# Side work paced closer together, and buffers and weights placed elsewhere, in a hybrid decoder step

## The chip, the cores and the metric

The kernel runs on one core of a Trainium2 chip. The metric is the device time of one execution in microseconds (us). A core has TensorE (PE, matmuls, with a separate record PEld for weight loads), VectorE (DVE), ScalarE (ACT), GpSimd (POOL) and SyncE (SP, which issues most DMAs). Each engine takes its instructions in the order of the built program and waits on semaphores for the others. Intermediate results of PE go to accumulators (`acc`, `tp`, `po`), from which DVE and ACT fetch them.

## The reference

One layer of a decoder with 1024 model dimensions, for a prompt of 2048 tokens and 8 samples of one token each, all in fp32:

```python
ada = silu(c) @ w_ada + b_ada
shift, scale, gate = split(ada, 3)
hn = rmsnorm(x, g_norm) * (1 + scale) + shift
xa, za, q, k, v, glr, zg = split(hn @ w_in)
...
xc = conv_b + sum(xp[:, j:j + T] * conv_w[j] for j in range(4))   # RG-LRU group, from xa
gx, ga = sigmoid(blockdiag(xc, w_gate_x)), sigmoid(blockdiag(xc, w_gate_a))
h = linear_recurrence(a(ga), mult * gx * xc)
y_lru = h * silu(za)
...
o, S = gated_linear_attention(q, k, v, log_alpha(glr))            # GLA group, 4 heads
y_gla = rmsnorm(o) * silu(zg)
...
x = x + gate * (concat(y_lru, y_gla) @ w_out)
y = rmsnorm(x, g_final)
```

The outputs are `y` for prompt and samples and the new states (recurrence, convolution, attention). So there are two large products, the input projection `hn @ w_in` and the output projection by `w_out` (2048 x 1024), and everything between is per head or per tile of 128 channels.

## The kernel before, in words

**Arithmetic.** A product of fp32 matrices is made of three matmuls in a reduced-precision type (fp32r): both operands are split into a high part, a cast on ACT, and a low part, a subtraction on DVE (`hh` and `hl` for the data, two halves of `w` for the weights), and high x high, high x low and low x high are summed in an accumulator. Split weights are made once and stored in DRAM (`parts`).

**Stages.** Tokens are worked in two halves. In the first half, tokens 0 to 1023, the attention heads run in the order 3, 0, 1, 2 and after each head some LRU tiles. From about 598 to 709 us stands a stage that computes the second half's gate columns (`zg` of three heads, `za` and `xa` of two tiles) in a Strassen-like way: `seven` makes a 2 x 2 block product of seven products instead of eight (five of them with sums or differences of blocks on one side). The data's sums come from `sums` (`so`, `ra`), the weights' differences from `pair_weights`. `gates_ahead` and `gates_seven` put the results through SiLU (ACT L1096, DVE L1097) into buffers `zs` and store them (`zgd`), `lru_seven` runs a whole LRU tile with its scan (DVE L1294) and output (DVE L1312). Then follows the second half: heads, and after each one LRU tile; tiles 6 and 7 come last. Last comes the output phase, from about 1190 us, again with seven products per block pair (L1792), whose weights `w<-wd` (L1656) and data `a<-mixd` (L1908) are loaded from DRAM and, where not stored split, cast on ACT (L1642).

**Side work and its pacing.** Three jobs run in the background: `ada_gate` (the adaLN gate), `pair_weights` (five pairs of column blocks of `w_in`: load at L749, two groups of differences at L753, four split copies at L758 and L759 with their stores at L763) and `out_weights` (16 steps over `w_out`: load at L809, two multiplications by the gate and four differences at L827, for every second group of four steps two split copies at L831 and L832, and stores to `wd` and `wd2` at L845 and L836). A step of `out_weights` uses one buffer `r`, so the next load can land only when the last step's stores have been read. `out_weights` begins when both other jobs are done (`ready`). None of this is placed by hand: each part ends with `after(units, fn)`, which puts its successor on a heap, due when a clock has advanced by so many units; the main loops call `tick`, which advances the clock and runs what is due. So the delays written in the jobs set how many steps fit into a stage. `with behind(V)` puts an instruction after the last that DVE has been given so far. `out_weights` pauses for the stage of sevens, whose pool `sp` takes the place of its buffers (pool `hp`): `lru_last_a` sets a stop flag and `close_sp` resumes. A scheduler decides the final order on each engine from this program.

At the end of the second half's loop stand these lines (L1624); what is left of `out_weights` is run there, ahead of the output phase's first loads and, in SP's and ACT's order, of the gates of LRU tile 6 (PE L1275 to L1277, whose input `xh` ACT casts at L1255):

```python
    while outw["busy"]:
        heapq.heappop(pend)[2]()
```

**Buffers of the stage of sevens.** `new_zs` hands out four shared buffers of pool `lp`, used by the gates and by the LRU tiles alike. Pool `sp` has slots s0 to s5; `fs4` holds the blocks' sums in s0, s1 and s2. Weights of a product are a tile of 2 x 1088 floats per partition that holds two operands, loaded by `operand` at float 0 and 576, or, for products whose data is a sum (`shifted`), at 48 and 560; `ra` starts at float 48 of a row of 1088.

The other lines that matter below: the projections' weight loads L302, PE L650 to L652 and L335 to L337 (projection matmuls), L1354 (eviction of the LRU input), L1514 (the matmul of `product`), L1528 (an eviction between two of the seven products).

Of the kernel before, what the change touches and what calls it, by code (L numbers as in the profile page):

```python
# [54 lines left out]
def hybrid_kernel(ctx, tc, i, o):  # L55
# [685 lines left out]
    def pair_weights(n=0):  # L741

        cols = zpairs()
        if n == len(cols):
            ready("pairs")
            return
        r = hp.tile([P, 2, KT, P], F32, tag="tr", name="tr")
        for a, col in enumerate(cols[n]):
            SP.dma_start(r[:, a], i["w_in"][0, :, col:col + P].rearrange("(k p) n -> p k n", p=P))  # L749
        b11, b21, b12, b22 = r[:, 0, :4], r[:, 0, 4:], r[:, 1, :4], r[:, 1, 4:]  # L750

        def sub(x, y, z):
            return lambda: V.tensor_tensor(x, y, z, op=OP.subtract)  # L753

        def split(k, x):
            def f():
                t = hp.tile([P, 4, P], F32R, tag="th", name="th", bufs=2)
                S.copy(t, x)  # L758
                V.tensor_tensor(x, x, t.bitcast(F32), op=OP.subtract)  # L759

                def store():
                    for u, y in enumerate((t.bitcast(F32), x)):
                        SP.dma_start(twd[n, k, :, u], y.rearrange("p k n -> p (k n)"))  # L763

                after(0.5, store)
            return f

        def one(ops):
            if not ops:
                after(1, lambda: pair_weights(n + 1))  # L770
                return
            with behind(V):
                for f in ops[0]:
                    f()
            after(0.5, lambda: one(ops[1:]))

        after(1.5, lambda: one([[sub(b11, b12, b11), sub(b12, b22, b12)], [sub(b22, b22, b11), sub(b21, b21, b22)]]
                               + [[split(k, x)] for k, x in enumerate((b11, b22, b12, b21))]))

    def out_weights(s0=0):  # L780


        def begin(s):
            q = s // 8
            outw["busy"] = True

            g = hp.tile([P, 2, 256], F32, tag="g", name="g")
            bt = hp.tile([P, 2, 256], F32, tag="t", name="bt")
            SP.dma_start(g, dram(gated, (8 + 32 * q) * 256, [[0, P], [64 * 256, 2], [1, 256]]))
            SP.dma_start(bt, dram(i["b_ada"], 2 * D + q * 256, [[0, P], [512, 2], [1, 256]]))  # L790
            r = load(s)

            def add():
                with behind(V):
                    V.tensor_tensor(g, g, bt, op=OP.add)
                after(0.5, lambda: step(s, r, g))

            after(4, add)

        def where(s):  # L800

            return s // 8, s // 4 % 2, s % 4

        def load(s):
            q, f, m = where(s)
            r = hp.tile([P, 2, 2, 256], F32, tag="r", name="r")
# [12 lines left out]

        def step(s, r, g):  # L820
            t = hp.tile([P, 3, 256], F32, tag="t", name="t")
            b11, b12, b21, b22 = r[:, 0, 0], r[:, 0, 1], r[:, 1, 0], r[:, 1, 1]
            q, f, m = where(s)
            c = slice(q * 256, q * 256 + 256)

            def op(*a):
                return lambda: V.tensor_tensor(*a[:3], op=a[3])  # L827

            def split(n, x):
                p = hp.tile([P, 2, 256], F32R, tag="p", name="p", bufs=2)  # L830
                S.copy(p[:, 0], x)  # L831
                V.tensor_tensor(p[:, 1], x, p[:, 0].bitcast(F32), op=OP.subtract)  # L832

                def store2():
                    for h in range(2):
                        SP.dma_start(wd2[n, :, h, m, c], p[:, h].bitcast(F32))  # L836

                after(1.5, store2)

            def store():  # L840

                for x, ops in ((r[:, 0], (B11, T1)), (r[:, 1], (B21, B22)), (t, (T2, T3, T4))):
                    for n, k in enumerate(ops):
                        if not (f and k in (B22, T4)):
                            SP.dma_start(wd[f, k, :, m, c], x[:, n])  # L845
                if outw["stop"] or s == 15:
                    outw["busy"], outw["next"] = False, s + 1
                elif s % 8 < 7:
                    after(1, lambda: again(s + 1, g))
                elif q == 0:  # L850
                    after(1, lambda: begin(s + 1))

            one([[op(r[:, 0], r[:, 0], g, OP.mult)], [op(r[:, 1], r[:, 1], g, OP.mult)],
                 [op(t[:, 1], b22, b12, OP.subtract), op(b12, b12, b11, OP.subtract)],
                 [op(t[:, 0], b22, b12, OP.subtract), op(t[:, 2], b21, t[:, 0], OP.subtract)]]
                + ([[lambda: split(0, b22)], [lambda: split(1, t[:, 2])]] if f else []), lambda: after(1, store))

        def again(s, g):
            r = load(s)
            after(1.5, lambda: step(s, r, g))  # L860

        begin(s0)
# [560 lines left out]
        ra[:] = [new_ra(F32) for _ in range(2)]  # L1423

    def new_ra(dt):
        return wp.tile([P, 1088], dt, tag="wr", name="ra")[:, 48:1072].rearrange("p (k t) -> p k t", k=2)

    def new_so(n):
        return sp_.tile([P, 4, 512], F32R, tag=f"s{n}", name="so")
# [54 lines left out]
    operands = []  # L1484

    def operand(src, shifted):

        if operands:
            c = 560 if shifted else 576
            w = operands.pop()  # L1490
        else:
            c = 48 if shifted else 0
            w = wp.tile([P, 2, 1088], F32R, tag="w", name="w", bufs=3)
            operands.append(w)
        w = w[:, :, c:c + 512]
        SP.dma_start(w.bitcast(F32), src)
        return w.rearrange("p u (k n) -> p u k n", k=4)
# [22 lines left out]
    def seven(n, use, c2, first=False):  # L1520
# [6 lines left out]
        y = acc()  # L1527
        S.copy(y, x)  # L1528
        if first:
            product(x, ZB21, n, False)  # L1530
            use(0, 0, x)
            g = acc()
            product(g, ZT4, n, True)
            gs = xp.tile([P, 512], F32, tag="f512", name="gs")
            S.copy(gs, g)
        e = acc()
# [25 lines left out]
    def gates_seven(n):  # L1562

        h = HEADS[1 + n]

        def use(dt, s, ps):
            z = new_zs()
            silu(z, ps)
            S.dma_start(zgd[2 * h + dt][:, s * 512:s * 512 + 512], z)

        seven(n, use, lambda s: new_zs(), n == 0)

    def lru_seven(j):
        xa_load, xa_new, xa_unit, out = lru_units(1, seven=True)
# [630 lines left out]
```

## Time and profile before

| | |
|---|---|
| three runs | 1521.42, 1521.81, 1523.98 us; median 1521.81 |
| the profiled execution | 1517.38 us, of which 1515.6 us is the span |
| mean granted clock of TensorE | 0.977 |
| chain that ended last | PE 78%, DVE 8%, ACT 5%, DMA 5% |
| `pair_weights` copies (ACT L758) | 20, from 134.0 to 334.3 us |
| `out_weights` multiplications (DVE L827) | 32 in 16 steps, from 405.9 to 1139.6 us |
| stage of sevens (PE L1514) | 599.6 to 708.9 us |
| first matmul of the output phase (PE L1792) | 1190.49 us |

The span is the time from the first to the last instruction of the profiled execution; all times of rows are from its start. A row of a timeline has the start, the duration, engine, line and operation, the output and input tiles, a count where neighbours were put together, and in brackets how long the engine had been idle before it and what released it. A row of waits reads: engine and instruction that waited, what released it, total us, times, longest. The page shows the span in 40 slices of 37.9 us, a digit being tenths of busy time.

### The profile page before, as it was taken

The numbers are of one execution on the slowest core, as the hardware profiler recorded it, in microseconds if no ns is written. First come the engines' busy times: TensorE is split into PE (matmuls) and PEld (weight loads), VectorE is DVE, ScalarE is ACT, GpSimd is POOL, SyncE is SP. The second block draws the span as 40 slices with busy tenths as digits, with TensorE's granted clock in tenths as the row PEclk, the third lists the DMA queues.
The fourth block names the chain that finished last, engine by engine and source line by source line (L and its number), as shares of the span: only waits on it lengthen the run. The fifth ranks groups of instructions, "written<-read, shape, count | busy, mean of one in ns | idle before, by whom it ended". The sixth has DMA issues, their size and how long they took to land.

```text
span 1515.6 us, 23410 instructions
## 1 busy us (share of the span) xinstructions
PE 1429.4 (94%) x8693; PEld 1249.2 (82%) x8693; DVE 1052.1 (69%) x2471; ACT 692.4 (46%) x1253; POOL 30.1 (2%) x44
## 2 busy tenths in 40 slices
PE   8999999999999999998999999999905999999998
PEld 6888889989899887777999999999804887778886
DVE  5767666765765687744387785868746896588886
ACT  4654535553552567334345555354405632144332
POOL 1200000000000002000000000000000100000000
PEclk9999999999999999999999999999956999999999
DMA  9656766764554634767557465664563658793452
GB/s 328 247 174 222 258 201 210 239 221 158 180 181 150 233 126 146 253 215 253 198 181 228 139 201 157 202 203 166 162 198 125 257 190 296 241 353 131 153 170 112
DMA packets 206135, 305.31 MB, mean 201 GB/s; under 512 B 13570, under 2 KB 143778, under 8 KB 203581
## 3 DMA queue, kind: packets, MB, share of 16 engines
q1 hardware_dynamic: 171317, 282.58, 55.6%
q10 hardware_dynamic: 34352, 20.19, 4.3%
q8 instruction: 68, 1.11, 0.3%
q0 software_dynamic: 352, 1.05, 0.2%
q14 instruction: 46, 0.38, 0.1%
HBM read 188.51 MB, written 115.33 MB: 200 GB/s over the span
## 4 chain that ended last, share of the span: by engine, by line
PE 78%; DVE 8%; ACT 5%; DMA 5%; issue 2%; SPq 1%; POOL 0%; DVEq 0%; ACTq 0%; POOLq 0%
PE acc L1792 12%; PE acc L650 10%; PE acc L652 10%; PE acc L651 10%; PE tp L1792 8%; PE acc L1514 5%; PE acc L335 4%; PE acc L336 4%; PE acc L337 4%; PE po L1044 1%; DMA r<-in_w_out_dram 1%; PE tp L1130 1%; DVE tg L1294 1%; PE tp L1010 1%; PE acc L1275 1%
## 5 line engine op out<-in xcount | busy, mean ns | idle before, releaser
L650 PE MATMUL acc<-hh,w 128*128 128x512 f32 (+3 forms) x1096 | 383.4, 350 | 1.8 <-DMA w<-parts 1.5
L651 PE MATMUL acc<-hl,w 128*128 128x512 f32 (+3 forms) x1096 | 372.9, 340 | 0.7 <-DVE hl L202 0.6
L652 PE MATMUL acc<-hh,w 128*128 128x512 f32 (+3 forms) x1096 | 372.5, 340 | 0.0
L650 PEld LDWEIGHTS acc<-hh,w 128*128 128x128 f32 x1096 | 206.2, 188 | 20.9 <-DVE f L973 1.8
L651 PEld LDWEIGHTS acc<-hl,w 128*128 128x128 f32 x1096 | 206.3, 188 | 19.0 <-DVE hl L202 1.9
L652 PEld LDWEIGHTS acc<-hh,w 128*128 128x128 f32 x1096 | 206.1, 188 | 17.4 <-issue 0.4
L1792 PE MATMUL acc<-w,a 128*128 128x512 f32 (+1 forms) x792 | 184.8, 386 | 0.0
L1792 PEld LDWEIGHTS acc<-w,a 128*128 128x128 f32 x792 | 146.8, 188 | 33.2 <-issue 3.4
L335 PE MATMUL acc<-w,hh 128*128 128x256 f32 (+1 forms) x508 | 145.4, 286 | 4.1 <-DVE zs L1097 4.0
L337 PE MATMUL acc<-w,hl 128*128 128x256 f32 (+1 forms) x508 | 143.4, 282 | 0.2 <-DVE hl L225 0.2
L336 PE MATMUL acc<-w,hh 128*128 128x256 f32 (+1 forms) x508 | 143.2, 282 | 0.0
L1792 PE MATMUL tp<-w,a 128*128 128x512 f32 x564 | 136.0, 391 | 0.0
L1792 PEld LDWEIGHTS tp<-w,a 128*128 128x128 f32 x564 | 105.2, 188 | 26.8 <-issue 5.2
L335 PEld LDWEIGHTS acc<-w,hh 128*128 128x128 f32 x508 | 96.3, 190 | 6.5 <-DVE zs L1097 4.2
L337 PEld LDWEIGHTS acc<-w,hl 128*128 128x128 f32 x508 | 96.7, 190 | 0.4 <-DVE hl L225 0.4
L336 PEld LDWEIGHTS acc<-w,hh 128*128 128x128 f32 x508 | 96.2, 189 | 0.1
L1096 ACT ACTIVATE zs<-acc 128x512 f32<-128x512 f32 (+3 forms) x73 | 36.8, 505 | 119.9 <-PE acc L652 104.4
L1275 PE MATMUL acc<-xh,wg 128*128 128x512 f32 (+3 forms) x80 | 31.2, 392 | 57.8 <-ACT xh L1255 57.1
L1642 ACT CAST a<-s 128x512 fp32r<-128x512 f32 x61 | 36.5, 619 | 95.8 <-issue 36.2
L1238 DVE SCALAR_TENSOR_TENSOR cv<-xa,vecT,cv 128x512 f32<-128x512 f32 (+2 forms) x120 | 75.7, 638 | 5.9 <-ACT cv L1236 5.5
L1097 DVE SCALAR_TENSOR_TENSOR zs<-zs,acc 128x512 f32<-128x512 f32 (+3 forms) x73 | 41.5, 568 | 51.4 <-ACT zs L1096 51.4
L1275 PEld LDWEIGHTS acc<-xh,wg 128*128 128x128 f32 x80 | 15.6, 197 | 63.7 <-ACT xh L1255 57.4
(373 smaller groups left out, 2555.1 us busy)
## 6 DMA issues: line engine op xcount, KB each, us to landing
parts<-w SPq DMA_DIRECT2D x37, 1024.0 KB
w<-parts SPq DMA_DIRECT2D x28, 1024.0 KB
wr<-in_w_in_dram SPq DMA_DIRECT2D x44, 512.0 KB
a<-mixd SPq DMA_DIRECT2D x63, 256.0 KB
w<-wd SPq DMA_DIRECT2D x12, 1024.0 KB
w<-twd SPq DMA_DIRECT2D x20, 512.0 KB
mixd<-zs ACTq DMA_DIRECT2D x34, 256.0 KB
wada<-in_w_ada_dram SPq DMA_DIRECT2D x16, 512.0 KB
```

Source lines behind the costliest of these rows:

```text
L335: PE.matmul(ps, hh[:, kt, c], hi[:, kt % 4], start=kt == 0, stop=False)
L336: PE.matmul(ps, hh[:, kt, c], lo[:, kt % 4], start=False, stop=False)
L337: PE.matmul(ps, hl[:, kt, c], hi[:, kt % 4], start=False, stop=kt == KT - 1)
L650: PE.matmul(ps[:, :n], hi[:, kt], a, start=kt == 0, stop=False)
L651: PE.matmul(ps[:, :n], hi[:, kt], b, start=False, stop=False)
L652: PE.matmul(ps[:, :n], lo[:, kt], a, start=False, stop=kt == KT - 1)
L1096: S.activation(z, ps, AF.Tanh, scale=0.5)
L1097: V.scalar_tensor_tensor(z, z, 1.0, ps, op0=OP.add, op1=OP.mult)
L1238: V.scalar_tensor_tensor(cv[:, cq], xa[:, cq.start + k:cq.stop + k], cw[k], cv[:, cq], op0=OP.mult, op1=OP.add)
L1275: PE.matmul(ps, wgh[:, g], xh[:, c], start=True, stop=False)
L1514: PE.matmul(ps, w[:, u, k], x[v][k], start=start and (k, u, v) == (0, 0, 0), stop=(k, u) == (3, 1), skip_group_check=True)
L1792: PE.matmul(ps, t[:, u, k], w[:, v, k, c], start=(q < 3 or ps is own) and (k, u, v) == (0, 0, 0), stop=(k, u) == (3, 1), skip_group_check= ...
```

## The change

1. In `pair_weights` the four split copies are issued two at a time, and the next pair begins at once instead of after 1 unit. In `out_weights` the two multiplications are issued together, then the four differences together, then both split copies together; the waits before the stores of split copies (1.5 to 0.5 units), before the stores (1 to 0.5) and before the next step (1 to 0.5) are shorter.
2. In `gates_seven`, for all gates but the first head's, results go to a tile `zq` of four turns in slot s2 of pool `sp` instead of the shared buffers.
3. Weights of products with sums, and `ra`, start eight floats later.
4. In `seven` for the first head, the product ZT4 is written ahead of ZB21.

```diff
@@ pair_weights
             if not ops:
-                after(1, lambda: pair_weights(n + 1))
+                pair_weights(n + 1)
                 return
...
-        after(1.5, lambda: one([[sub(b11, b12, b11), sub(b12, b22, b12)], [sub(b22, b22, b11), sub(b21, b21, b22)]]
-                               + [[split(k, x)] for k, x in enumerate((b11, b22, b12, b21))]))
+        halves = [split(k, x) for k, x in enumerate((b11, b22, b12, b21))]
+        after(1.5, lambda: one([[sub(b11, b12, b11), sub(b12, b22, b12)], [sub(b22, b22, b11), sub(b21, b21, b22)],
+                                halves[:2], halves[2:]]))
@@ out_weights
-                after(1.5, store2)
+                after(0.5, store2)
...
-                    after(1, lambda: again(s + 1, g))
+                    after(0.5, lambda: again(s + 1, g))
                 elif q == 0:
-                    after(1, lambda: begin(s + 1))
+                    after(0.5, lambda: begin(s + 1))
...
-            one([[op(r[:, 0], r[:, 0], g, OP.mult)], [op(r[:, 1], r[:, 1], g, OP.mult)],
-                 [op(t[:, 1], b22, b12, OP.subtract), op(b12, b12, b11, OP.subtract)],
-                 [op(t[:, 0], b22, b12, OP.subtract), op(t[:, 2], b21, t[:, 0], OP.subtract)]]
-                + ([[lambda: split(0, b22)], [lambda: split(1, t[:, 2])]] if f else []), lambda: after(1, store))
+            one([[op(r[:, 0], r[:, 0], g, OP.mult), op(r[:, 1], r[:, 1], g, OP.mult)],
+                 [op(t[:, 1], b22, b12, OP.subtract), op(b12, b12, b11, OP.subtract),
+                  op(t[:, 0], b22, b12, OP.subtract), op(t[:, 2], b21, t[:, 0], OP.subtract)]]
+                + ([[lambda: split(0, b22), lambda: split(1, t[:, 2])]] if f else []), lambda: after(0.5, store))
@@ new_ra
-        return wp.tile([P, 1088], dt, tag="wr", name="ra")[:, 48:1072].rearrange("p (k t) -> p k t", k=2)
+        return wp.tile([P, 1088], dt, tag="wr", name="ra")[:, 56:1080].rearrange("p (k t) -> p k t", k=2)
@@ operand
-            c = 560 if shifted else 576
+            c = 568 if shifted else 576
...
-            c = 48 if shifted else 0
+            c = 56 if shifted else 0
@@ seven
         if first:
+            g = acc()
+            product(g, ZT4, n, True)
             product(x, ZB21, n, False)
             use(0, 0, x)
-            g = acc()
-            product(g, ZT4, n, True)
@@ gates_seven
+        def new():
+            if n == 0:
+                return new_zs()
+            zturn[0] += 1
+            return zq[0][:, zturn[0] % 4]
+
         def use(dt, s, ps):
-            z = new_zs()
+            z = new()
...
-        seven(n, use, lambda s: new_zs(), n == 0)
+        if n == 1:
+            zq[:] = [sp_.tile([P, 4, 512], F32, tag="s2", name="zq")]
+        seven(n, use, lambda s: new(), n == 0)
```

More of the change, by code (lines that the diff above doesn't have):

```diff
@@ L1482, in sums @@
             drips.append(lambda n=n, u=u: step(n, u))
-    operands = []
+    operands, zq, zturn = [], [], [0]
     def operand(src, shifted):
         if operands:
-            c = 560 if shifted else 576
+            c = 568 if shifted else 576
             w = operands.pop()
         else:
-            c = 48 if shifted else 0
+            c = 56 if shifted else 0
             w = wp.tile([P, 2, 1088], F32R, tag="w", name="w", bufs=3)
```

## The prediction

> **What bounds the kernel now.** I read the page from the top, then the waits, then the stretches where the waits sit.
>
> ```profile
> span 1515.6 us, 23410 instructions
> PE 1429.4 (94%) x8693; PEld 1249.2 (82%) x8693; DVE 1052.1 (69%) x2471; ACT 692.4 (46%) x1253; POOL 30.1 (2%) x44
> PE   8999999999999999998999999999905999999998
> ...
> PEclk9999999999999999999999999999956999999999
> ```
>
> PE is busy 94% of the span and 9 in nearly every slice, so the kernel is bound by TensorE except where a slice is lower: one slice is 0 and the next 5, and the granted clock drops there and there alone. The waits of PE name it:
>
> ```profile
> PE acc L1275 <- ACT xh L1255: 57.1, 1, 57.1
> PE acc L335 <- DVE zs L1097: 4.0, 1, 4.0
> PE tp L209 <- DVE x L181: 2.2, 3, 1.7
> ```
>
> One wait of 57.1 us, one of 4.0 us, then nothing over 2.2 us in total. So a change that leaves the matmuls as they are can win some 61 us at two places, and crumbs elsewhere. The table of stretches (time, PE, PEld, DVE, ACT, POOL busy, granted clock, DMA share, GB/s) shows what the rest has to spare:
>
> ```profile
> 200.00:300.00 100.00, 99.86 (x631) 90.50 (x630) 69.08 (x152) 46.70 (x85) 0.00 (x0) 1.00 0.65 209
> ...
> 900.00:1000.00 100.00, 98.55 (x774) 94.41 (x774) 74.57 (x237) 49.95 (x103) 0.00 (x0) 1.00 0.62 193
> ...
> 1100.00:1150.00 50.00, 0.00 (x0) 0.00 (x0) 20.50 (x43) 3.24 (x8) 0.00 (x0) 0.50 0.63 206
> ```
>
> From 1100 to 1150 us PE does nothing while DVE works 20.5 of 50 us and ACT 3.2. What runs there is on DVE:
>
> ```profile
> 1098.92 1.52 DVE L827 TENSOR_TENSOR r<-r,g 128x512 f32<-128x512 f32 x2 [4.21 <-DMA r<-in_w_out_dram]
> ...
> 1138.59 0.69 DVE L827 TENSOR_TENSOR r<-r,g 128x512 f32<-128x512 f32 x1 [3.76 <-DMA r<-in_w_out_dram]
> ```
>
> These are the last six of the 16 steps of `out_weights`, run one after another by the loop that empties the heap when the second half ends. Each step is load, wait some 4 us, compute 3 to 4 us, store, and the next load needs the buffer: (1138.59 - 1098.92) / 5 = 7.9 us a step. Then come the loads and casts for the output phase, and only then the gates of tile 6:
>
> ```profile
> 1145.73 0.32 SPq L1656 DMA_DIRECT2D w<-wd  x1
> ```
>
> ```profile
> 1150.84 1.14 ACT L1642 CAST w<-w 128x512 fp32r<-128x512 f32 x2 [8.18 <-DMA w<-wd]
> ```
>
> ```profile
> 1096.18 0.34 PE L652 MATMUL acc<-hh,w 128*128 128x384 f32 x1
> 1153.63 1.01 PE L1275 MATMUL acc<-xh,wg 128*128 128x384 f32 x2 [57.11 <-ACT xh L1255]
> ...
> 1160.77 0.39 PE L650 MATMUL acc<-hh,w 128*128 128x264 f32 x1
> ```
>
> **The change, part by part. Part 1, the steps sooner.** The work per step is unchanged. Only its ticks of the pacing clock go: a pair's split pieces go two at a time, a pair's successor comes at once, and an out-weight step takes two or three turns instead of four to six, with shorter delays. In the built program seven of the 16 steps lie ahead of the second half instead of three, and the nine others lie spread through it at what are now 766 to 1035 us, 25 to 37 us apart. The last store of out-weights is SP instruction 529 of 705, in front of the last weight loads of the projections; the emptying loop finds nothing. Six steps leave the gap.
>
> What takes their place: PE has its last matmul of tile 6's projection at 1096.18 + 0.34 = 1096.5, and the next projection starts at 1160.8, 64.2 us later. In between stand 18 gate matmuls, 12 of 384 columns and 6 of 264. At full clock neighbouring projection matmuls follow one another at:
>
> ```profile
> 1094.97 0.33 PE L651 MATMUL acc<-hl,w 128*128 128x384 f32 x1
> 1095.14 0.33 PE L652 MATMUL acc<-hh,w 128*128 128x384 f32 x1
> ...
> 1161.61 0.28 PE L650 MATMUL acc<-hh,w 128*128 128x264 f32 x1
> 1161.73 0.28 PE L651 MATMUL acc<-hl,w 128*128 128x264 f32 x1
> ```
>
> 12 x 0.17 + 6 x 0.12 = 2.8 us. The gates' inputs still pass through ACT, which now has casts of out-phase weights mixed in: from the built order, with a cast at half of the 1.14 us above, I estimate some 8 us of ACT work between 1091 and 1099, and so 2.4 us of waiting for PE. So 5.2 us instead of 64.2: **-59.0**. The bounds are 2.8 us, no wait at all (-61.4), and 2.8 + 2.4 + 8.2 = 13.4 us, ACT blocked for a whole weight load as in the row at 1150.84 (-50.8). I take the inner value: in the built order the `w<-wd` load stands behind the load below, waits only on transfers long done, and has some 15 us before its cast.
>
> ```profile
> 1075.46 0.53 SPq L302 DMA_DIRECT2D w<-parts  x1
> 1088.29 0.53 SPq L302 DMA_DIRECT2D w<-parts  x1
> ```
>
> What it costs: four steps move into the first half and two more into the body of the second. By form a step is two multiplications, four subtractions and, for every second group of four, two more on DVE and two casts on ACT:
>
> ```profile
> L827 DVE TENSOR_TENSOR r<-r,g x32: 679/684/693, 405.9 to 1139.6; 128x512 f32<-128x512 f32 x32
> L827 DVE TENSOR_TENSOR t<-r x32: 414/420/427, 411.9 to 1141.3; 128x256 f32<-128x256 f32 x32
> ```
>
> 2 x 0.68 + 4 x 0.42 = 3.0 us, with the split 3.9: 12 to 15 us of DVE more in some 250 us of a first half where, by the row of 200 to 300, DVE has 31 of 100 us free. The row of 900 to 1000 bounds what fuller engines cost: with DVE at 74.6% PE still does 98.6, so 200 us at its 1.45% idle instead of none would be 2.9 us. Bursts of 1.7 us in front of an eviction, instead of 0.8, sit inside that. New in kind: with two casts back to back, the second two of a pair need the two `th` buffers that the first two's stores still read. Below, nothing; above, five pairs, each holding ACT (and PE behind it) for as long as the longest semaphore wait in the row:
>
> ```profile
> L758 ACTq EVENT_SEMAPHORE  x20: 17/17/2297, 133.0 to 332.9; - x20
> ```
>
> 5 x 2.3 = 11.5 us. One such wait need not reach PE, whose accumulators are double, so I stay near the lower end: **+2.0** for everything in part 1, bounds 0 and +14.4 (11.5 + 2.9).
>
> **Part 2, gate buffers in a free slot.** In the 4.0-us wait, PE needs an accumulator that SiLU frees; SiLU's product is queued on DVE behind a 2.3-us scan:
>
> ```profile
> 711.70 2.34 DVE L1294 TENSOR_TENSOR_SCAN tg<-xl,hc,tx 128x1024 f32<-128x1024 f32 x1
> ...
> 715.35 0.68 DVE L1097 SCALAR_TENSOR_TENSOR zs<-zs,acc 128x512 f32<-128x512 f32 x1
> ```
>
> ```profile
> 716.09 0.39 PE L335 MATMUL acc<-w,hh 128*128 128x272 f32 x1 [4.01 <-DVE zs L1097]
> ...
> 717.28 0.43 PE L335 MATMUL acc<-w,hh 128*128 128x272 f32 x1
> 717.50 0.43 PE L336 MATMUL acc<-w,hh 128*128 128x272 f32 x1
> ...
> 720.34 0.29 PE L335 MATMUL acc<-w,hh 128*128 128x272 f32 x1
> 720.47 0.29 PE L336 MATMUL acc<-w,hh 128*128 128x272 f32 x1
> ```
>
> The wait also halved the clock from 716.6 to 720.0: matmuls 0.22 apart instead of 0.13, some 15 of them, 1.5 to 1.7 us. The SiLU that holds the accumulator waits for a shared buffer that the LRU tile's output (two products at 714.15, ahead of the one at 715.35) gives back; from the free slot it doesn't, and its product goes ahead of the scan. What is late next: an ACT eviction of the value tile, whose place overlaps the slot, waits for the SiLU's store; I leave PE 1.6 us there. So -(4.0 - 1.6) - 1.7 = -4.1, and -0.4 from the 0.37 wait on a shared buffer at 671.59 below: **-4.5**. Bounds: -6.1 (4.0, 1.7 and 0.4 in full), and +2.9 if the eviction waits for a store like the SiLU at 717.32 did:
>
> ```profile
> 671.59 0.73 PE L1514 MATMUL acc<-so,w 128*128 128x512 f32 x2 [0.37 <-DVE zs L1097]
> ```
>
> ```profile
> 717.32 0.60 ACT L1096 ACTIVATE zs<-acc 128x512 f32<-128x512 f32 x1 [2.93 <-DMA mixd<-zs]
> ```
>
> The clock's row first: a 4.0-us wait cost the full clock, none of the waits under 2.3 us did. The Trainium skill, "TensorE: Matmul & The Clock Gate", section "What's actually happening", says the same with a window: the clock falls to half after an idle window of about 3.4 us and returns after a busy one. The trace agrees: the half clock lasted 3.4 us here. By that rule a remaining wait that crosses the window would leave the 1.7 us where they are and make the part -2.8.
>
> **Part 3, weights eight floats on.** A run of 24 products with sums (`so`) takes longer than plain ones:
>
> ```profile
> 605.45 0.50 PE L1514 MATMUL acc<-hh,w 128*128 128x512 f32 x1 [0.66 <-ACT acc L1528]
> ...
> 613.45 5.86 PE L1514 MATMUL acc<-so,w 128*128 128x512 f32 x24 [1.16 <-ACT gs L1535]
> 619.15 0.39 PE L1514 MATMUL acc<-hh,w 128*128 128x512 f32 x1
> ...
> 665.12 0.62 PE L1514 MATMUL acc<-hh,w 128*128 128x512 f32 x2
> ...
> 668.52 0.39 PE L1514 MATMUL acc<-hh,w 128*128 128x512 f32 x1
> ```
>
> The first matmul after a wait lasts 0.50 instead of 0.39, so (619.15 - 613.45 - 0.11) / 24 = 233 ns for `so`, against (668.52 - 665.12) / 15 = 227 in a plain run of 15. Worked out from the two programs' tile places, plain products have data and weights at the same byte modulo 128, `so` products have data at 96 and weights at 64; after the change both are at 96. 160 of `so` and 20 of `ra` by 6 ns: **-1.1**, bounds -1.1 and +1.1 (a shift that makes the mismatch the other way). The Trainium skill speaks against this part: "TensorE: Matmul & The Clock Gate", section "Step-by-step: what each phase is for", gives PE two independent read ports, so that loading weights takes nothing from the running matmul. By that rule the part is worth 0 and the sum 1.1 us higher; the 6 ns of the rows speak for some conflict.
>
> **Part 4, one product moved in the source.** In the built program PE's matmuls keep their order; only one weight load is issued some 30 us later, still 3 us before its use. **0**, bounds -0.7 and +0.7, the 0.66-us accumulator wait of the row at 605.45, at that place.
>
> **Sum.** -59.0 + 2.0 - 4.5 - 1.1 + 0 = **-62.6 us**. The profiled execution took 1517.4 us (span 1515.6 and 1.8 around it), so 1454.8 on its scale. The three runs' median, 1521.8, lies 4.4 us above it; on their scale the forecast is **1459.2 us**.
>
> **Rivals.**
> (a) *The gap closes only in part.* SP is in order; if `w<-wd` gets stuck behind the load at 1088.29, the casts hold ACT for the 8.2 us of the row at 1150.84, and the clock falls with it, up to 2.8 us more (the 18 matmuls once again). 1467 to 1470. For it: ACT takes the casts ahead of the gates' `xh`. Against: that load's place in the order.
> (b) *Split copies stall.* Five pairs hold ACT for 2.3 us each and fuller engines take 2.9: 1459.2 + 14.4 - 2.0 = 1472. For it: two buffers, four copies. Against: PE at 99.9 in the row of 200 to 300, in which such copies run, with ACT at 47, shows cover.
> (c) *The other side: bursts stall DVE.* Grouped steps put a multiplication on DVE that waits in place for its load, as in the gap, 4.2 us, with evictions queued behind it. If each of the 16 steps did and PE ran dry each time, 16 x 4.2 = 67.2 us: 1459.2 + 67.2 = 1526. It decides from 62.6 / 4.2 = 15 steps. Against: of the ten steps outside the gap none shows DVE idle for its load, and the delay between load and multiplication is not cut.
> (d) *It doesn't do what it says.* Each step left for the emptying loop costs 7.9 us: 1467 with one. Against: the built order.
>
> **How the numbers follow.** Forecast with its inner uncertainty (1452 to 1465): 0.72. (a) 0.12, (b) 0.08, (d) 0.03, (c) 0.03, and 0.02 for half of (c), no change. The low end takes all favourable bounds, -61.4 + 0 - 6.1 - 1.1 - 0.7 = -69.3, 1452.5, and 2.5 for the spread of such runs (1521.4 to 1524.0): 1450. The high end takes in (a), (b) and two left-over steps: 1476; both (a) and (b) in full would be 1482 to 1485 and are left out. This kernel's measurement can tell about 0.2%, 3 us, from no change. Faster 0.95, same 0.02, slower 0.03.
>
> **What would show it.** Part 1: no PE wait over 5 us, clock 1.0 at the end of the second half, no multiplication of L827's kind without PE beside it; wrong if a `w<-wd` wait of 8 us stands there. Its cost: PE share of 100 to 600 us under 99%, or an ACT wait on `th`. Part 2: the 4.0-us wait under 2, and no half clock near 716. Part 3: `so` products at 227 ns; wrong if they stay at 233. Part 4: no new wait near 605. The forecast fails if several places of the first half lose a microsecond each.

## The result, and the profile after

| | before | after |
|---|---|---|
| median of four executions | 1522.7 us | 1479.7 us (1478.7 to 1483.1) |
| ratio, 95% interval | | 0.972 [0.970, 0.974] |
| profiled execution, span | 1517.4, 1515.6 | 1483.1, 1481.3 |

The change makes the kernel 43.0 us faster; forecast were 62.6, and the time lies above the range (1450 to 1476). The two profiled executions lie 34.3 us apart, because that of before was a quick one (its executions beside all the runs took 1517.4 to 1527.8) and that of after the slowest of its four. What follows compares traces with traces, and keeps medians for the verdicts. Lines behind the edits stand further down in the changed kernel: L809, L845, L1173 and L1514 of before are L810, L846, L1174 and L1515.

The page of the changed kernel, the same lines as before:

```profile
span 1481.3 us, 23382 instructions
...
PE 1432.7 (97%) x8693; PEld 1253.9 (85%) x8693; DVE 1050.7 (71%) x2471; ACT 691.2 (47%) x1253; POOL 30.0 (2%) x44
...
PE   8999999999999999999899999798999999999998
...
PEclk9999999999999999999999999899999999999999
```

The empty slice is gone, as forecast. But three slices (of 37.0 us each) stand at 8, 7 and 8: those from 704, 926 and 1000 us. The first answers to the 8 that the kernel before has there; the other two are new. The waits of PE say what stands there (columns: times total, number, longest):

```profile
PE acc L650 <- DMA w<-parts: 14.1, 3, 8.0
PE tp L878 <- DVE g L872: 3.0, 1, 3.0
PE acc L651 <- DVE hl L202: 2.7, 2, 2.5
...
PE acc L1276 <- ACT tx L1279: 2.2, 1, 2.2
PE tp L1011 <- DVE xb L996: 2.1, 2, 1.1
...
PE acc L335 <- DVE zq L1098: 1.3, 1, 1.3
```

The 57.1 us are gone, and 14.1 us of waiting for the projection's weight loads stand in their place where there were 1.5: 2.5 at 845, 8.0 at 942 and 3.6 at 1037. Two rows of the table by stretches answer to those of before:

```profile
200.00:300.00 100.00, 99.86 (x625) 90.13 (x624) 72.00 (x156) 47.47 (x87) 0.00 (x0) 1.00 0.74 240
...
900.00:1000.00 100.00, 91.61 (x698) 88.06 (x697) 68.48 (x225) 45.66 (x97) 0.00 (x0) 0.95 0.58 184
```

In the first half PE stands at 99.86 as before, with DVE at 72 instead of 69. From 900 to 1000, PE falls from 98.6 to 91.6 with DVE less busy than before: it isn't DVE's load that slows this stretch.

Matching the matmuls of the two traces one by one gives how late each is in the changed kernel (us; the start-up's difference is taken off; the head of the table is the matmul's time before):

| 450 | 560 | 597 | 612 | 709 | 735 | 905 | 950 | 1010 | 1040 | 1096 | 1161 | end |
|---|---|---|---|---|---|---|---|---|---|---|---|---|
| +2.1 | +1.4 | +4.7 | +5.1 | +4.0 | +6.0 | +8.7 | +18.5 | +18.4 | +24.0 | +23.7 | -34.6 | -34.9 |

The gap is worth -58.3 (from +23.7 to -34.6). What the forecast lacks is paid before it, in steps: 2.1 by 450, 3.3 at 560 to 597, 2.0 at 709 to 735 where 4.5 were to be won, 9.8 at 905 to 950 and 5.6 at 1010 to 1040.

The 2.1 us by 450 are the two waits of PE for `xb` in the list above, 1.0 us at 190 and 1.1 at 453. Each time DVE works off side work first; at 453 it is the four differences of an out-weight step, 1.7 us:

```profile
450.51 0.41 DVE L828 TENSOR_TENSOR t<-r 128x256 f32<-128x256 f32 x1
...
452.23 0.68 DVE L996 SCALAR_TENSOR_TENSOR xb<-acc,xb 128x512 f32<-128x512 f32 x1
```

The gap itself, PE in the changed kernel:

```profile
1120.59 0.33 PE L652 MATMUL acc<-hh,w 128*128 128x384 f32 x1
...
1124.17 0.44 PE L1276 MATMUL acc<-xh,wg 128*128 128x384 f32 x1 [2.21 <-ACT tx L1279]
...
1126.83 0.39 PE L650 MATMUL acc<-hh,w 128*128 128x264 f32 x1
```

From the last projection matmul's end (1120.9) to the next projection are 5.9 us, forecast 5.2, with a wait of 2.2, forecast 2.4.

The largest new loss, SP around the weight load that comes late, and PE after it:

```profile
925.22 1.32 SPq L1174 DMA_DIRECT2D zs<-zgd  x2
926.63 2.17 SPq L846 DMA_DIRECT2D wd<-r  x3
...
930.36 0.92 SPq L846 DMA_DIRECT2D wd<-t  x2
932.66 1.22 SPq L810 DMA_DIRECT2D r<-in_w_out_dram  x2
933.92 1.26 SPq L302 DMA_DIRECT2D w<-parts  x2
```

```profile
941.91 0.66 PE L650 MATMUL acc<-hh,w 128*128 128x384 f32 x1 [8.04 <-DMA w<-parts]
942.37 0.52 PE L651 MATMUL acc<-hl,w 128*128 128x384 f32 x1
942.69 0.52 PE L652 MATMUL acc<-hh,w 128*128 128x384 f32 x1
```

PE was ready at 941.91 - 8.04 = 933.9; the load was issued at 933.92, behind seven stores and two loads of an out-weight step. The matmuls after the wait stand 0.32 apart instead of 0.17 until 946: half clock, 12 matmuls, 1.8 us more. In the kernel before the same weight load was issued 5.5 us ahead of its use, and its two loads of `w_out` stood behind it (SP, before):

```profile
912.45 0.32 SPq L1173 DMA_DIRECT2D zs<-zgd  x1
...
919.06 0.64 SPq L302 DMA_DIRECT2D w<-parts  x1
921.47 0.32 SPq L836 DMA_DIRECT2D wd<-p  x1
921.88 1.26 SPq L809 DMA_DIRECT2D r<-in_w_out_dram  x2
```

There it came just in time: PE's semaphore wait for it ended at 924.46, the first matmul on it started at 924.59, and no idle time of note stands before it. This load has no slack, so whatever SP does ahead of it is paid in full.

### The profile page after: what moved, and what is told of

Read it like the earlier page. It is cut to its first block, busy times and chain, and to the rows that moved or that the text cites. A ratio compares the mean times of both kernels' runs of the same rounds, so it can differ in the third digit from the quotient of the medians.

```text
span 1481.3 us, 23382 instructions
## 1 busy us (share of the span) xinstructions
PE 1432.7 (97%) x8693; PEld 1253.9 (85%) x8693; DVE 1050.7 (71%) x2471; ACT 691.2 (47%) x1253; POOL 30.0 (2%) x44
## 4 chain that ended last, share of the span: by engine, by line
PE 77%; DVE 11%; DMA 6%; ACT 4%; issue 2%; SPq 0%; POOL 0%; ACTq 0%; DVEq 0%
PE acc L1801 12%; PE acc L650 10%; PE acc L651 10%; PE acc L652 10%; PE tp L1801 9%; PE acc L1515 5%; PE acc L335 3%; PE acc L336 3%; PE acc L337 3%; DMA w<-parts 3%; PE po L1045 1%; DVE cv L1239 1%; PE tp L1131 1%; DMA tr<-in_w_in_dram 1%; PE acc L1276 1%
## 5 line engine op out<-in xcount | busy, mean ns | idle before, releaser
L650 PE MATMUL acc<-hh,w 128*128 128x512 f32 (+3 forms) x1096 | 385.4, 352 | 14.4 <-DMA w<-parts 14.1
L928 ACT CAST vh<-acc 128x256 fp32r<-128x256 f32 x56 | 20.7, 371 | 89.1 <-PE acc L337 71.1
L929 DVE TENSOR_TENSOR vl<-acc,vh 128x256 fp32r<-128x256 f32 x56 | 23.5, 420 | 51.5 <-ACT vh L928 51.4
```

Source lines behind the costliest of these rows:

```text
L650: PE.matmul(ps[:, :n], hi[:, kt], a, start=kt == 0, stop=False)
```

## The experiments

Three theories of the missing time were set against each other. **Queue**: SP is in order, and out-weight steps put their stores and loads, and the waits of these, ahead of weight loads. **Engines**: the grouped operations on DVE and ACT delay what PE needs. **Traffic**: the DMA engines are fuller, and the loads take longer wherever they are issued. Runs are told in the order of the questions. Medians are beside the kernel before on the same chip, whose own median was 1522.3 to 1524.4.

### The parts alone

**Part 1 alone** (parts 2 to 4 as before).

```diff
+ part 1's hunks in pair_weights and out_weights
- part 2's, 3's and 4's hunks in new_ra, operand, seven and gates_seven
```

> Part 1 alone, on the kernel before. Both theories give nearly the whole gain to part 1. Queue theory (the missing 20 us are weight loads that SP issues late, because stores and loads of out-weight steps stand ahead of them): the two waits of PE for w<-parts near 925 and 1015 us stay, 8 and 4 us, and the time is 1479 to 1483. Part 2 won 3.9 us at 716 and lost 3.9 us behind it again, so without it the time is the same within 3 us; if part 2 did pay as forecast (4.5 us), it is 1484 or more.

Measured: 1483.4 us, ratio 0.974 [0.972, 0.976]. The two waits for `w<-parts` stay (9.4 us, longest 6.6). The gain is part 1's. By the medians parts 2 to 4 bring 3.7 us on top of part 1 (1479.7, ratio 0.970 to 0.974, so the intervals overlap), by the traces nothing; this run does not decide between the two.

**Parts 2, 3 and 4 alone** (part 1's hunks as before).

> Parts 2, 3 and 4 alone. If the slot's gain is given back by the value tile's eviction, which waits for the gate stores, 1520.5 to 1522 (part 3 alone shows, -1.1 us); if the forecast of the parts held, -5.6 us, 1517.

Measured: 1525.8 us over twelve executions, ratio 1.0023 [1.0011, 1.0036]: 3 us slower, which neither number said. In the trace the wait at 716 falls from 4.0 to 1.3 and 3.9 us are won from 709 to 720, but by 735 all of it is lost again (+0.6 in all), and 2.6 more by 950, in waits for just-in-time weight loads.

**Parts 3 and 4 alone.**

> Parts 3 and 4 alone. so products 227 ns apart instead of 233, 180 of them: -1.1 us, 1520.5 to 1521.5; if the eight floats don't matter, 1521.8 and 233 ns as before.

Measured: 1522.0 us, ratio 1.000 [0.999, 1.001]. The matmuls with sums, first before, then in this run (durations: shortest, median, longest), and a new wait:

```profile
L1514 PE MATMUL acc<-so,w x160: 388/394/505, 611.9 to 699.5; 128*128 128x512 f32 x160
```

```profile
L1514 PE MATMUL acc<-so,w x160: 388/389/501, 612.1 to 698.5; 128*128 128x512 f32 x160
```

```profile
606.57 0.47 PE L1514 MATMUL acc<-hh,w 128*128 128x512 f32 x1 [2.04 <-DMA w<-parts]
```

Part 3 does what it was to do: the median duration falls from 394 to 389 ns, the mean time from one start to the next from 233 to 228 ns (for `ra` from 231 to 228). That makes 160 x 4.9 + 20 x 2.5 ns = 0.8 us; 0.7 are seen in the trace from 613 to 709. The runs below that leave part 4 out have the same 228 ns, and part 1 alone has 233. Part 4: the weight load that it moves is now issued at 601.6 and used at 606.57 after a wait of 2.0, where a wait of 0.66 for an accumulator stood. By 613 the two waits behind it have shrunk by as much, and nothing of it is left. Together nothing that can be measured.

### Out-weight steps and the gap

**The out-weight half of part 1 alone.**

```diff
- one([[sub(...), sub(...)], ..., halves[:2], halves[2:]])     # pair_weights as before
+ out_weights grouped and with the shorter delays, as in the change
```

> Only the out-weight half of part 1, on the kernel before: pair copies keep their old pace, so out-weight steps start later and in the built order one of the 16 is left for the emptying loop, with one more just ahead of it. If each left-over step costs its 7.9 us and pair copies cost next to nothing: 1483.4 (part 1 alone) + 8 = 1491. If the grouped pair copies cost 3 us or more of the first half, those 3 come off: 1488 or less.

Measured: 1499.9 us, ratio 0.985 [0.982, 0.988], 9 us above the number. Its trace loses nothing by 450 us (+0.0; part 1 whole: +1.8). That difference is not the paired copies' alone. Every run with the paired copies loses 0.6 to 1.0 us by 200, this one nothing. The 1.1 us at 453 are gone here, but also in the next run, which keeps the paired copies and has small groups (+0.4 by 450). The one step left over costs more than 7.9, PE's wait at the gates of tile 6:

```profile
PE acc L1275 <- ACT xh L1255: 12.8, 1, 12.8
```

**Old small groups at half the delay**, from the changed kernel.

```diff
- [op(r[:, 0], ...), op(r[:, 1], ...)], [four differences]] + [[both splits]]
+ [op(r[:, 0], ...)], [op(r[:, 1], ...)], [two], [two]] + [[split], [split]]
- after(0.5, (lambda: one(ops[1:], end)) ...
+ after(0.25, (lambda: one(ops[1:], end)) ...
```

> The changed kernel with the operations of an out-weight step issued in the old small groups (0.7 to 1.4 us of DVE at a time), at half the old delay. Paired copies stay. In the built order three steps are left for the emptying loop: by the two runs with one left over (12.8 and 9.8 us of waiting) and 7.9 for each further one, 1479.7 + 26 = 1506. If the bursts were what costs 1 us near 450 us and more in the second half, those losses go and it is 1500.

Measured: 1501.7 us, ratio 0.986 [0.984, 0.988]. The three steps left over make PE wait as long as this:

```profile
PE acc L1276 <- ACT xh L1256: 35.2, 1, 35.2
```

With one step left 12.8 (and 9.8 in the run with a pause below), three 35.2, six 57.1. The first costs 10 to 13 us, not 7.9, since the output phase's first loads and casts stand behind it; from one to six it is (57.1 - 12.8) / 5 = 8.9 a step. The time is near the 1500 that was to speak for bursts, and by 450 us the loss has indeed gone from 2.1 to 0.4. For the second half the run does not part group size from place: smaller groups also change what stands ahead of a weight load on SP. There PE waits for no weight load. All on SP, the run has, from 900 to 1000:

```profile
900.00:1000.00 100.00, 99.57 (x778) 95.70 (x777) 72.32 (x235) 50.30 (x101) 0.00 (x0) 1.00 0.57 183
```

PE at 99.6 instead of 91.6. Until the gap the run is 2.9 us late where the changed kernel is 23.7.

### Late weight loads: queue, traffic or place

**Loads and stores of out-weight steps on POOL's queue.**

```diff
- SP.dma_start(r[:, a], i["w_out"]...)   SP.dma_start(wd2[...], ...)   SP.dma_start(wd[...], ...)
+ G.dma_start(r[:, a], i["w_out"]...)    G.dma_start(wd2[...], ...)    G.dma_start(wd[...], ...)
```

> The changed kernel, with the loads and stores of out-weight steps issued by POOL instead of SP; engine work is the same. Queue theory: the w<-parts waits of 8 and 4 us go with their clock losses, 15 us less than the changed kernel, about 1465. Engine theory (grouped bursts on DVE and ACT delay evictions and PE waits for those): the waits come back under another name, 1477 to 1481. Bandwidth theory (the loads land late because the DMA engines are full): as the engine theory in time, but the loads are issued earlier and land as late.

Measured: 1470.6 us, ratio 0.966 [0.964, 0.968]: 9 of the 15 us. The 8.0-us wait and its half clock are gone, the one near 1037 is 2.5 instead of 3.6. SP at the same load:

```profile
921.19 1.31 SPq L1174 DMA_DIRECT2D zs<-zgd  x3
924.15 1.89 SPq L302 DMA_DIRECT2D w<-parts  x2
```

From the first of the `zs` loads to the weight load 3.0 us instead of 8.7. Engine work is the same, and its cost did not come back under another name: the engine theory fails at this place. The bandwidth theory (traffic) does not fail everywhere. The wait that is left belongs to a load that POOL's queue did not help: issued at 1013.66, it landed 8.1 us later.

```profile
1013.66 1.88 SPq L302 DMA_DIRECT2D w<-parts  x2
```

```profile
1021.85 0.41 PE L650 MATMUL acc<-hh,w 128*128 128x384 f32 x1 [2.51 <-DMA w<-parts]
```

**Only the stores on POOL's queue; only the loads on POOL's queue.** These two move the same traffic and part the queue's two contents.

```diff
- SP.dma_start(wd2[...], ...)   SP.dma_start(wd[...], ...)       # first run
+ G.dma_start(wd2[...], ...)    G.dma_start(wd[...], ...)
- SP.dma_start(r[:, a], i["w_out"]...)                           # second run
+ G.dma_start(r[:, a], i["w_out"]...)
```

> The changed kernel with only the stores of out-weight steps on POOL's queue; the loads of w_out stay on SP. The traffic is the same. Queue theory: SP still has to wait in place at the load of w_out until the step's stores have landed, since it takes the same buffer, so the weight loads behind it near 934 us are issued at most 1 us earlier: the 8.0-us wait stays at 6 to 8, 1478 to 1480. If it were only the number of entries on SP (seven stores, 4 us), it falls to 4 and the time to 1474. Bandwidth theory: 8 us whatever the queue, but then the run with both on POOL's queue should not have lost that wait.

> The changed kernel with only the loads of w_out on POOL's queue; the stores stay on SP, in the same order. Queue theory: SP goes on to the weight loads right after the last store, 1.4 us of waiting and 1.2 us of two issues earlier: the 8.0-us wait falls to about 5.4, the one near 1038 by 1.2, and the time to about 1475. Bandwidth theory: no change, 1479 to 1480.

Measured: 1478.6 [ratio 0.969 to 0.974] and 1477.8 [0.969 to 0.973]. The stores' run, SP and PE:

```profile
925.39 1.71 SPq L1174 DMA_DIRECT2D zs<-zgd  x3
928.42 1.54 SPq L810 DMA_DIRECT2D r<-in_w_out_dram  x2
930.02 1.26 SPq L302 DMA_DIRECT2D w<-parts  x2
```

```profile
937.96 0.66 PE L650 MATMUL acc<-hh,w 128*128 128x384 f32 x1 [2.94 <-DMA w<-parts]
```

The loads' run:

```profile
921.61 1.17 SPq L1174 DMA_DIRECT2D zs<-zgd  x2
...
927.47 1.48 SPq L302 DMA_DIRECT2D w<-parts  x2
```

```profile
933.83 0.41 PE L650 MATMUL acc<-hh,w 128*128 128x384 f32 x1 [3.30 <-DMA w<-parts]
```

| run | `zs` to weight load on SP | weight load to use | wait |
|---|---|---|---|
| changed kernel | 8.7 | 8.0 | 8.0 |
| stores moved | 4.6 | 7.9 | 2.9 |
| loads moved | 5.9 | 6.4 | 3.3 |
| both moved | 3.0 | 5.7 | none |

Each takes about 5 us of the wait, where I had said 1 and 2.6 (1 us of the stores' 5 because PE itself comes later). Two things add up: the entries delay the issue (column 2), and a weight load right behind the 512 KB of `w_out` takes 8 us instead of 5 to 6 (column 3). So it is queue and traffic. That the 512 KB stand on the same queue is not what makes the load slow: in later runs with these loads on POOL's queue (the two 'POOL's queue' runs below with the other buffer, and the fastest one) single weight loads took 8.0 to 8.7 us to land. What ahead of a load makes it slow isn't shown in detail; with the same neighbours, one near 924 took 5.5 us in one run and 8.0 in another. In the time only 1 and 2 us of the gain are seen, within the intervals; the wait near 1037 and the losses of the first half stay.

**A pause after the sixth step.** The losses from 560 to 597 have another cause: the seventh step runs into the stage of sevens, and the loads of `x` wait for its buffers.

```diff
- if outw["stop"] or s == 15:
+ if outw["stop"] or s == 15 or s == 5:
```

> The changed kernel with out-weight steps paused after the sixth, so that the seventh does not run into the stage of sevens, where the loads of x wait for its buffers. If that is the cause of the 2.5-us and 0.8-us losses near 575 us, they go (the loads of x are issued before 530 us again) and ten steps stand in the second half: 1476 if they fit, 1479.7 - 3.6 + 8 = 1484 if one is left over. If the late loads of x are not the cause, the losses near 575 stay.

Measured: 1493.9 us, ratio 0.980 [0.979, 0.982]. The last three loads of `x`, first in the changed kernel (all five together), then here:

```profile
550.30 3.52 SPq L253 DMA_DIRECT2D xst<-in_x_prompt_dram  x5
```

```profile
527.04 2.37 SPq L253 DMA_DIRECT2D xst<-in_x_prompt_dram  x3
```

The 3.3 us are gone (+1.9 at 560, +1.9 at 597): the seventh step is shown to be the cause; that it acts through the late loads of `x` is read from the trace. But one step of the ten is left over (9.8 us), and the weight load near 845 is waited for 6.0 us instead of 2.5: +3.6 ahead of it, +11.7 at 905. It lost more than the pause won, and 10 us more than the 1484 that was expected with one step left.

**The pause with a shorter delay behind the loads, all on SP; and on POOL's queue** with the other buffer (below) and part 4 undone.

```diff
+ if outw["stop"] or s == 15 or s == 5:
- after(1.5, lambda: step(s, r, g))
+ after(1, lambda: step(s, r, g))
```

> The changed kernel with the same pause and shorter delay, all loads and stores on SP as in the changed kernel. Losses near 575 gone (-3.6), nothing left over; but ten steps in the second half on SP's queue. Queue theory: two or three weight loads are still late, 10 to 18 us, 1476 to 1485, and at least 10 us more than the same thing on POOL's queue. Engine theory: 1476, within 4 us of the version on POOL's queue once that version's other two edits (about 3 us) are counted.

> The version with POOL's queue, the other buffer and part 4 undone, and now a pause after the sixth step, with 1 unit instead of 1.5 between a step's load and its multiplications so that the ten others end as early as nine did. The loads of x come early and nothing is left over: 1468.9 - 3.6 = 1465. If the shorter delay makes DVE wait for its loads, each step costs up to 2 us more and it is 1470 or above.

Measured: 1482.0 us, ratio 0.973 [0.971, 0.975], on SP, and 1475.4 [0.966 to 0.971] on POOL's queue. Nothing is left over and the 575 loss is gone in both. But 10 us of difference that the queue theory wanted are 6.5, some 3 of them the other two edits', and both runs have 7.2 us of waits for `w<-parts`, whatever the queue, with ten steps in the second half instead of nine. So the queue alone is not the cause either. The run on POOL's queue is 10 us above its 1465; the condition named for 1470 or above came true, since multiplications waited for their loads (4.6, 1.6 and 2.2 us of DVE, against none in the changed kernel; the run on SP has three such waits of 1.2 to 1.7). How much of that reached PE isn't shown.

**A slower second half.** Eight steps in the first half (by the shorter delay), eight in the second in small groups at half the delay; the other buffer; part 4 undone. First all on SP, then on POOL's queue.

```diff
+ if s0: ops = one or two operations each
- after(0.5, (lambda: one(ops[1:], end)) ...
+ after(0.25 if s0 else 0.5, (lambda: one(ops[1:], end)) ...
- after(1.5, lambda: step(s, r, g))
+ after(1, lambda: step(s, r, g))
```

> All on SP, part 4 undone and the other buffer for the last gate results; in the first half groups as in the changed kernel and a shorter delay behind the load, so that eight steps are done there, in the second half the old small groups at half the delay, eight steps at a slower pace. Position theory (what makes a weight load late is a whole step's stores and next load standing right ahead of it, not how many steps there are): as in the ungrouped run no weight load is late in the second half, about 1479.7 - 15 - 3.9 - 1 = 1460 to 1464. Traffic theory: eight steps instead of nine save at most two ninths of the 15 us, 1472 or more.

> The same with out-weight loads and stores on POOL's queue. Position theory: no weight load is late in either, so the same as on SP within 3 us, 1460 to 1465. If SP's entries still cost, 3 us or more below the run on SP.

Measured: 1467.7 us, ratio 0.964 [0.962, 0.966], and 1463.2, ratio 0.962 [0.959, 0.964]. On SP the waits for `w<-parts` are 3.9 us in all instead of 14.1, with eight steps instead of nine: far more than two ninths. Place counts, though the time is above the 1460 to 1464 of the position theory: the eighth step runs into the stage of sevens, and PE waits there 4.5 us again. Small groups came with the new place in this run, so the two are not parted by it; in the first run on POOL's queue the 8.0-us wait went with the large groups kept. POOL's queue still brings 4.5 (the intervals overlap a little). The last is the fastest version found, 16.5 us below the changed kernel. Its PE:

```profile
PE 1430.8 (98%) x8693; PEld 1251.0 (85%) x8693; DVE 1050.4 (72%) x2470; ACT 691.8 (47%) x1253; POOL 122.8 (8%) x204
...
PE   8999999999999999999999999998999999999998
```

### Where part 2's gain went

In the changed kernel PE's wait at 716 shrank as forecast, to 1.3, with no half clock. What came then, ACT:

```profile
719.89 0.55 ACTq L1576 DMA_DIRECT2D zgd<-zq  x1
...
728.92 0.37 ACT L928 CAST vh<-acc 128x256 fp32r<-128x256 f32 x1 [8.23 <-DMA zgd<-zq]
```

The value tile takes the slot's place, so its first eviction waits until the gates' last store, 256 KB issued at 719.89, has landed: 8.9 us later. The likely reason lies on SP, which had issued 2 MB of the data's blocks and some 2 MB of weights just before; no run takes these loads away to test it:

```profile
708.59 0.53 SPq L1627 DMA_DIRECT2D hh<-a21d  x1
709.17 0.95 SPq L1627 DMA_DIRECT2D hl<-a21d  x1
...
711.31 3.48 SPq L302 DMA_DIRECT2D w<-parts  x2
```

Behind ACT's wait PE waits 3.0 us, and the half clock, gone from 716, comes here instead (matmuls 0.22 apart instead of 0.13 until 734.4):

```profile
730.41 0.16 PE L878 MATMUL tp<-ident,g 8*48 8x8 f32 x1 [3.01 <-DVE g L872]
...
731.25 0.43 PE L336 MATMUL acc<-w,hh 128*128 128x272 f32 x1
731.48 0.43 PE L337 MATMUL acc<-w,hl 128*128 128x272 f32 x1
```

**The last two gate results in another buffer.**

```diff
+ if n == 2 and zturn[0] >= 10:
+     return xp.tile([P, 512], F32, tag="f512", name="zl")
  zturn[0] += 1
```

> The changed kernel with the last two gate results of the stage in another buffer (the one for 512-float temporaries) instead of the free slot, so that the slot's last stores are issued some 8 us sooner. If the value tile's eviction waiting for those stores is what gave part 2's gain back, the 8.2-us wait of ACT and the 3.0-us wait of PE behind it go: 1479.7 - 3.9 = 1476. If the weight load and the reload of the data's blocks would have been late anyway, another wait takes their place: 1479 to 1480.

Measured: 1476.5 us, ratio 0.970 [0.967, 0.972]; the changed kernel's was 0.972, so 3 to 4 us less, as expected, at the edge of what the intervals tell. In the trace the stretch from 709 to 735 wins 4.2 us against the changed kernel, and the 3.0-us wait of PE is gone. That the eviction waited for the slot's last store is shown by the trace.

**It and POOL's queue together, part 4 undone.**

> The changed kernel with out-weight loads and stores on POOL's queue, the last two gate results in the other buffer, and part 4 undone. If the three causes are separate: 1470.6 - 3.9 - 1 = 1466. If the waits of the stage's end share a cause with full DMA engines, 1470.

Measured: 1468.9 us, ratio 0.965 [0.961, 0.968]; 1.7 below POOL's queue alone, where 4.6 were expected; the two intervals overlap nearly whole. The wait at 725 is gone, and 2.6 us are won from 709 to 735 against POOL's queue alone; a wait for `w<-parts` near 930 (2.4) is back, and 3.8 us are lost from 905 to 950.

## Why the forecast was right and wrong, step by step

- **The gap closes: right.** -59.0 forecast, -58.3 in the traces, with 5.9 us in its place instead of 5.2. The half clock went with it. Rival (a), the casts behind a late `w<-wd` load, didn't come.
- **"+2.0 for everything in part 1, bounds 0 and +14.4": the step that failed.** It measured +4.7 in the first half and +17.7 from 735 to 1096. The working priced DVE's bursts and ACT's split copies, and for these alone 2.0 came near (2.1 by 450), in part by luck. What cost was side work on DVE ahead of `xb`, two waits of 1.0 and 1.1 us. The stall of ACT that made the upper bound came once, 2.2 us for a store of `th` at 169, and did not reach PE. The working left out what a step issues on SP. I had the entries' durations in front of me (seven stores at some 0.4, two loads at 0.6, and the waits of both) and weighed SP's order only at the gap. What was needed was to ask at every weight load of the second half how long before its use it is issued: 5.5 us at the load near 919, of which 5.4 until it had landed. Late issue and slow landing cost 8.0 + 1.8 us there and some 5 at the next.
- **Part 1 in the first half, a step run into the stage of sevens.** The seventh step delays the opening of the next pool, and with it the loads of `x` by some 25 us; the forecast has no term for it. 3.3 us, shown by the pause.
- **Part 2: the mechanism right, the sum wrong.** -3.9 at 716, forecast -4.1; but "I leave PE 1.6 us there" for the eviction was too little. The store took 8.9 us, most likely since 4 MB of loads had been issued ahead of it. PE lost 0.9 us to a weight load at 722, 3.0 behind the eviction, and some 1.4 to the half clock after that, so the gain is gone by 735. The bound of +2.9 came from a wait for another store, at 717. The clock's reading also needs a correction: the half clock lasted 3.4 us, as forecast, but waits of 2.5 and 3.0 us, shorter than the idle window in the prediction, were enough to bring it (at 577 and 730).
- **Part 3: right in kind**, -1.1 forecast, -0.8 measured. By the Trainium skill ("TensorE: Matmul & The Clock Gate", section "Step-by-step: what each phase is for") the two read ports are independent, and loading weights takes nothing from the running matmul. 394 against 389 ns for 160 matmuls whose weights alone moved say that here the weights' address counts; by what mechanism isn't shown.
- **Part 4: 0 forecast, 0 left by 613.** But the weight load that I had 3 us before its use is waited for, 2.0 us instead of 0.7 for an accumulator, and only the shorter waits behind it make up for that.
- **Rivals.** (a) and (b) did not come, (c) neither: no multiplication waited for its load. (d): nothing was left over, but its price was too low, 10 to 13 us for the first step instead of 7.9. "Both (a) and (b) in full" would be 1480 to 1483, since the forecast's +2.0 was to be taken off there too. That the measured 1479.7 lies next to it is chance.

What stays open: why the store of `mixd` for which the `zs` load at 925 waits took 7.4 us to land (7.4 on POOL's queue too) instead of 4.0 in the kernel before; what makes one weight load land in 5.5 us and another in 8; and how much of the second half's losses an average execution has, since the traces differ by 34 us and the medians by 43.

## What to carry to other kernels

When background work is moved, list for each of its steps what it issues on every queue, and then, for each load that PE needs, how long before its use it is issued against how long it takes: where the two are equal, every entry put ahead of it is lost time, and the engine's free share says nothing about it. Look, for a transfer that something waits for, at what has been issued in the microseconds before it; the price of a like one in a quieter stretch was too low here (a 256-KB store 3.2 us, then 8.9). And a step that is left over at a stage's end costs its own time and that of everything that waits behind it.

## What the runs showed of the hardware

- A weight load of 1 MB landed 5.4 us after its issue in the kernel before (near 919) and 5.5 with an out-weight step's transfers on POOL's queue (near 924). Right behind 512 KB of `w_out` on the same queue it took 7.9 us, and 8.1 in the run on POOL's queue near 1014. A 256-KB store took 8.9 us to land with some 4 MB of loads issued in the 11 us before it, another, in the kernel before near 715, 3.2.
- Moving a step's DMAs from SP's to POOL's queue won 9 us. The Trainium skill ("DMA: Bandwidth & Descriptors", section "Issuing engines are not separate DMA queues") says that issuing from several engines saves only the sequencer's time to issue. Here that time is 5.7 us between two loads, and it holds the queue's waits as well. The landing was not always shorter on two queues (the 8.1 us near 1014).
- An 8.0-us wait of PE brought the half clock for 4 us (12 matmuls of 384 columns 0.32 us apart instead of 0.17), 1.8 us on top of the wait. Waits of 2.5 us (at 577), 3.0 (730) and 3.6 (1037) were each followed by 3.4 us of half clock; another of 2.5 (845) and one of 2.2 (1124) were not.
